# One ring of eight weight buffers, four split buffers and an even spread of the context's steps in a two-block network's expert stages

## The chip, the cores and the metric

The kernel runs on one NeuronCore of a Trainium2 chip. Its time is the device time of one execution in microseconds (us); lower is better. TensorE (PE) multiplies matrices, VectorE (DVE), ScalarE (ACT) and GpSimd (POOL) work on elements, and SyncE (SP) issues the DMA transfers that bring the weights from HBM into SBUF. Each engine takes its instructions strictly in the order in which they stand in its own queue.

## The reference, cut to what matters

Two blocks follow each other. The first runs on 256 tokens `x` of 1024 features: an RWKV layer and an attention layer, and behind each a mixture of experts. The second block begins with a feed-forward half-step on both `x` and a context `c` of 256 tokens; the context does not depend on the first block.

```python
def hier_moe(h, router_g, router_g_b, router_e, router_e_b, w_gate, w_up, w_down):
    # top-1 group of four, in it the top-2 of eight experts
    gates = ...                                   # (tokens, 4, 8), two of 32 not zero
    for gi in range(N_EXPERT_GROUPS):
        hid = jax.nn.silu(jnp.einsum('td,edf->tef', xt, w_gate[gi])) * jnp.einsum('td,edf->tef', xt, w_up[gi])
        hid = hid * gates[:, gi, :, None].astype(hid.dtype)
        out = out + jnp.einsum('tef,efd->td', hid, w_down[gi]).astype(f32)

def _ffn_half(h, g, shift, scale, gate, w_in, w_out):
    a, b = jnp.split(_modnorm(h, g, shift, scale) @ w_in, 2, axis=-1)
    return h + 0.5 * gate * ((jax.nn.silu(a) * b) @ w_out)
```

## The kernel before, in words

All weights lie in HBM as slots of 1 MiB (128 partitions of 2048 fp32). `K.slot` takes a buffer for the next slot and issues its DMA on SP's queue; `issue_after(self.last...)` chains the issues, so that the transfers are issued strictly in the order of the calls. An issue whose buffer is still being read waits, and all issues behind it wait too.

**An expert stage** (`moe`, called twice: after the RWKV layer, `moe0`, and after the attention layer, `moe1`) holds 96 expert slots: 32 experts in eight quads `q` = 0 to 7, 12 slots each. For a quad, `gate_up` multiplies eight slots into `ph` (line 1338, four matmuls of 512 columns a slot, fp32 weights read raw from the buffer). `experts` then computes `msg` = silu(gate) times up on ACT and DVE (lines 1399 and 1400), transposes it on PE into `cb` (line 1403; called T below), copies it to `hT` on ACT (line 1405), multiplies the four slots of the down projection into `py` (line 1411), and splits that into `yh` and `yl` on ACT and DVE (lines 1415 and 1416). After each odd quad 32 matmuls scatter the results of two quads back to the tokens (`cb`, lines 1425 and 1426), and DVE adds them to `X` (line 1427).

**The context's feed-forward half-step is the filler.** `side_ffn` is a generator of 33 steps in each expert stage, eleven times two input steps (`in_f_in`) and an output step (`in_f_out`). Each step takes one weight slot of its own and 48 matmuls of 256 columns. The product runs as three matmuls on pairs of a high and a low part (lines 135 to 137): a slot is split in four pieces of 512 columns, of each a high part `w` by a CAST on ACT (line 140) and a low part by a subtraction on DVE (line 141). The pieces live in the pool `spl`, two buffers. Two pairs of PSUM banks take the products (`fps`, `mps`). An input step ends with a silu on ACT (`sq`, line 343), a product on DVE (line 345) and the split of the result into `hh` (ACT) and `hl` (DVE), which the output step reads. `fill(n)` takes the next n steps; it is called after each second slot of `gate_up` and after the down projection, by the table `FILL` (a row for each quad, the fifth number after the down projection), and by `FRONT` in the first loads. The steps are emitted inside `tc.high_priority(offset=-30)`, which moves where the scheduler puts their instructions in the engines' queues relative to the experts'.

The expert slots rotate through the six buffers of the pool `mraw`, the context's slots through the three buffers of `K.raw`. When the first stage ends, `after()` computes the normalized input `u` of the context's next part (square sums, then for each of eight columns a product, `gs`, and the split `uh`, `ul`; lines 254 to 264). `load_ahead` issues the first slots of the following layer, and a branch (lines 1218 to 1220) skips the overflow loop.

Of the kernel before, what the change touches and what calls it, by code (L numbers as in the profile page):

```python
# [6 lines left out]
F32 = mybir.dt.float32  # L7
# [6 lines left out]
P = 128  # L14
# [12 lines left out]
class Pool:  # L27


    def __init__(self, pool, bufs, small):  # L30
        self.pool, self.bufs, self.small, self.sizes = pool, bufs, small, {}
# [23 lines left out]
@contextmanager  # L55
def sbuf(tc, name, bufs, small=False, side=None, **how):
    with tc.tile_pool(name=name, bufs=bufs, **how, **({"side": side} if side else {})) as p:
        q = Pool(p, bufs, small)
        yield q
        if not side:  # L60
            q.small = True
            q.align()


class Kern:


    def __init__(self, tc, ins, ctx):
        self.tc, self.nc, self.ins = tc, tc.nc, ins
        nc = self.nc  # L70
        ent = ctx.enter_context
        self.const = ent(sbuf(tc, reuse_waits="tile", name="const", small=True, bufs=1))
        self.raw = ent(sbuf(tc, reuse_waits="tile", name="raw", bufs=3))
        self.sm = ent(sbuf(tc, reuse_waits="tile", name="sm", small=True, bufs=2))
        self.nw = ent(sbuf(tc, reuse_waits="tile", name="nw", bufs=2))
        self.mp = ent(tc.tile_pool(reuse_waits="tile", name="mp", bufs=1, space=PSUM))
        self.const.pool.tile([P, 32], F32, name="first")
        self.ident = self.const.tile([P, P], F32, name="ident")
        nc.sync.dma_start(self.ident, ins["ident"])
        self.ones = self.const.tile([P, P], F32, name="ones")  # L80
        nc.vector.memset(self.ones, 1.0)
        self.last = self.spl = None
        self.ahead = {}

    def vec(self, name, n=8):
# [4 lines left out]
    def slot(self, stream, i, pool=None, to=None):  # L90
        if (stream, i) in self.ahead:
            return self.ahead.pop((stream, i))
        t = (pool or self.raw).tile([P, 2048], F32, name="raw") if to is None else to
        src = self.ins[stream][i]
        t = t[:, :src.shape[1]]
        if self.last and self.last[0] is self.nc.cur_bb:
            with self.tc.issue_after(self.last[1].ins):
                d = self.nc.sync.dma_start(t, src)
        else:
            d = self.nc.sync.dma_start(t, src)  # L100
        self.last = (self.nc.cur_bb, d)
        return t
# [1025 lines left out]
SOON = 60  # L1128

FRONT = (0, 0, 0, 0, 1, 1)  # L1130
FILL = [(0, 0, 0, 0, 1)] + [(1, 1, 1, 1, 1)] * 6 + [(0, 0, 0, 0, 0)]


def moe(K, mx, x, before, mods, gate, layer, s_w, side, after, ahead):

    nc, tc = K.nc, K.tc
    mm = nc.tensor.matmul
    with ExitStack() as ctx:
        mraw = ctx.enter_context(sbuf(tc, reuse_waits="tile", name="mraw", bufs=6 if side else 9))
        if side:  # L1140
            ctx.enter_context(K.splitting(2))
            ctx.enter_context(K.beside())
        ap = ctx.enter_context(sbuf(tc, reuse_waits="tile", name="mo1", small=True, bufs=1))
        loaded = {}

        def fill(n, late=30):
            with tc.high_priority(offset=-late):
                for _ in range(n if side else 0):
                    next(side, None)

        pos = ap.tile([P, 2, 32], F32, name="pos")
        gts = ap.tile([P, 2, 32], F32, name="gts")
        flag = ap.tile([P, 1], F32, name="flag")
        rt = ap.tile([P, 2], F32, name="rt")
        rw = ap.tile([P, 8, 36], F32, name="rw")
        nc.sync.dma_start(rw, K.ins["router"][layer])
        mc = ap.tile([P, 2 * P + 2 * 32 + 36 + 4], F32, name="mc")
        nc.sync.dma_start(mc, K.ins["moe_const"][layer])
        tri, iota, desc = mc[:, :P], mc[:, P:P + 32], mc[:, P + 32:P + 40]
        bias, sel4 = mc[:, P + 40:P + 76], mc[:, P + 76:P + 80]  # L1160

        def slot(i, to=None):
            if i in loaded:
                return loaded.pop(i)
            return K.slot(s_w, i, to=to, pool=None if 8 <= i % 12 < 11 and i < 84 and not side else mraw)


        gs, sh = mods
        rs = K.nw.tile([P, 8, 36], F32, name="sq")
        bt = ap.tile([P, 36], F32, name="bt")  # L1170
        nc.vector.tensor_mul(rs, rw, sh[:, :, None].to_broadcast([P, 8, 36]))
        nc.vector.tensor_mul(rw, rw, gs[:, :, None].to_broadcast([P, 8, 36]))
        ps = K.mp.tile([P, 36], F32, name="mps")
        for k in range(8):
            mm(ps, K.ones, rs[:, k], start=(k == 0), stop=(k == 7))
        nc.vector.tensor_add(bt, ps, bias)
        early = ExitStack()
        with tc.tile_pool(reuse_waits="tile", name="mop", bufs=1, space=PSUM) as pp, sbuf(tc, reuse_waits="tile", name="mo2", small=True, bufs=1) as wp:
            ps = pp.tile([P, 2, 36], F32, name="lp")
            ss = pp.tile([P, 2, 2], F32, name="ss")  # L1180
            before()
            xs = mx.tile([P, 8, 256], F32, name="m0")
            nc.gpsimd.tensor_copy(xs, x)
            lg = wp.tile([P, 2, 36], F32, name="lg")
            with tc.high_priority(offset=SOON):
                for k in range(8):
                    for t in range(2):
                        mm(ps[:, t], x[:, k, t * P:(t + 1) * P], rw[:, k], start=(k + t == 0), stop=(k == 7 and t == 1))
                K.square_sums(ss, x, 256)
                r = K.rsqrt_small(K.sm, ss[:, 0], 1.0 / 1024, EPS, 2, "rs")  # L1190
                nc.vector.tensor_copy(rt, r)
            for t in range(2):
                nc.vector.scalar_tensor_tensor(lg[:, t], ps[:, t], r[:, t:t + 1], bt, op0=OP.mult, op1=OP.add)
            gp = early.enter_context(sbuf(tc, reuse_waits="tile", name="mrt", bufs=1, side="right"))
            tokens = rows(K, gp, pp, x, rt)
            route(K, wp, lg, desc, pos, gts, pp, tri, flag)

        def between(b):
            for i in range(6 if side else 0):
                loaded[i] = slot(i)  # L1200
                fill(FRONT[i])
            for i in range(2):
                loaded[6 + i] = slot(6 + i, b[:, i])


        over = ap.tile([P, 8], F32, name="over")
        more = ap.tile([P, 1], I32, name="more")
        nc.vector.tensor_scalar(over, iota[:, :8], float(CAP), flag, op0=OP.mult, op1=OP.is_lt)
        nc.vector.tensor_reduce(flag, over[:, 1:], AX.X, OP.add)
        nc.vector.tensor_copy(more, flag)  # L1210
        dt = mx if layer else ap
        moe_round(K, dt, x, mods, gate, slot, pos, gts, iota, sel4, fill, between, (early, gp, tokens))
        fill(99)
        if after:
            after()
        K.load_ahead(ahead)
        with tc.issue_after(K.last[1].ins):
            n = nc.values_load(more[0:1, 0:1], min_val=0, max_val=7)
        with tc.If(n > 0):
            with tc.For_i(0, n):  # L1220
                nc.vector.tensor_scalar(pos, pos, -float(CAP), None, op0=OP.add)
                early = ExitStack()
                gp = early.enter_context(sbuf(tc, reuse_waits="tile", name="mrt", bufs=1, side="right"))
                with tc.tile_pool(reuse_waits="tile", name="mop", bufs=2, space=PSUM) as pp:
                    tokens = rows(K, gp, pp, xs, rt)
                moe_round(K, dt, x, mods, gate, slot, pos, gts, iota, sel4, lambda n: None, lambda b: None, (early, gp, tokens))
# [104 lines left out]
def gate_up(K, hp, slot, XT, q, fill):  # L1331

    ph = hp.tile([P, 512], F32, name="ph")
    for k in range(8):
# [5 lines left out]
        if k % 2:  # L1340
            fill(FILL[q][k // 2])
    return ph, m
# [48 lines left out]
def experts(K, wp, hp, x, gate, slot, phs, DT, XT, gsl, fill):  # L1391
    nc, tc = K.nc, K.tc
    mm = nc.tensor.matmul
    with tc.tile_pool(reuse_waits="tile", name="moe", bufs=1, space=PSUM) as pp, sbuf(tc, reuse_waits="tile", name="mor", bufs=2) as yp:
        ys = []
        for q in range(8):
# [20 lines left out]
            ys.append((yh, yl))  # L1417
            fill(FILL[q][4])
            if q % 2 == 1:
# [548 lines left out]
```

## Time and profile before

| | us |
|---|---|
| median of 3 runs | 3287.95 (3287.29 to 3293.46) |
| the profiled execution's own time | 3287.88 |
| its span in the profile | 3286.1 |
| first expert stage, first gate/up matmul to the last scatter | 752.2 to 1160.6 |
| second expert stage, the same | 1538.8 to 1949.6 |
| PE busy over the span | 3058.3 (93%) |
| DVE, ACT busy over the span | 1915.4 (58%), 1216.1 (37%) |
| mean of the DMA over the span | 199 GB/s |
| mean granted TensorE clock | 0.952 |

A view by windows gives, for a stretch of the span, the busy time of each engine with the number of its instructions, the granted clock, the mean busy share of the 16 DMA engines, and GB/s. A view of waits says which instruction waited for which, with the sum in us, the number of times and the longest. A row of the timeline is an instruction's start, its duration, engine, line, operation, output and inputs, and in brackets how long its engine had been idle before it and what ended that. The trace counts each matmul on raw fp32 weights twice, so a slot's four stand there as x8.

### The profile page before, as it was taken

The numbers are of one execution on the slowest core, as the hardware profiler recorded it, in microseconds if no ns is written. First come the engines' busy times: TensorE is split into PE (matmuls) and PEld (weight loads), VectorE is DVE, ScalarE is ACT, GpSimd is POOL, SyncE is SP. The second block draws the span as 40 slices with busy tenths as digits, with TensorE's granted clock in tenths as the row PEclk, the third lists the DMA queues.
The fourth block names the chain that finished last, engine by engine and source line by source line (L and its number), as shares of the span: only waits on it lengthen the run. The fifth ranks groups of instructions, "written<-read, shape, count | busy, mean of one in ns | idle before, by whom it ended". The sixth has DMA issues, their size and how long they took to land. (4 is left out here: it accounts for less than half of the span.)

```text
span 3286.1 us, 56989 instructions
## 1 busy us (share of the span) xinstructions
PE 3058.3 (93%) x23517; PEld 2490.1 (76%) x23517; DVE 1915.4 (58%) x4127; ACT 1216.1 (37%) x2560; POOL 212.7 (6%) x276
## 2 busy tenths in 40 slices
PE   5989999979998889999989979999999999999998
PEld 3765555566665579997666659999998888999998
DVE  4646665664444455555444448888865456544777
ACT  2532232233222245443322234455432223444443
POOL 1322232210000000000000000000000000000000
PEclk7889898989999989998999989999999999999999
DMA  7556676646888733345688764444532222232443
GB/s 262 190 193 220 228 267 212 244 178 263 339 324 328 303 126 142 129 146 233 273 339 322 309 254 185 172 165 170 190 116 90 103 90 91 103 105 101 167 181 115
DMA packets 98623, 654.59 MB, mean 199 GB/s; under 512 B 10672, under 2 KB 19760, under 8 KB 20400
## 3 DMA queue, kind: packets, MB, share of 16 engines
q1 hardware_dynamic: 95920, 648.73, 52.6%
q8 instruction: 188, 3.08, 0.4%
q10 hardware_dynamic: 2432, 2.10, 0.2%
q14 instruction: 83, 0.68, 0.1%
HBM read 649.74 MB, written 1.05 MB: 198 GB/s over the span
## 5 line engine op out<-in xcount | busy, mean ns | idle before, releaser
L140 ACT CAST w<-raw 128x512 fp32r<-128x512 f32 x1184 | 671.8, 618 | 760.9 <-issue 305.1
L141 DVE TENSOR_TENSOR w<-raw,w 128x512 fp32r<-128x512 f32 x1184 | 774.8, 688 | 291.8 <-ACT w L140 287.2
L135 PE MATMUL ab<-uh,w 128*128 128x258 f32 (+2 forms) x1440 | 446.3, 310 | 8.4 <-ACT uh L216 4.5
L136 PE MATMUL ab<-ul,w 128*128 128x258 f32 (+2 forms) x1440 | 446.3, 310 | 1.2 <-DVE ul L217 0.8
L137 PE MATMUL ab<-uh,w 128*128 128x258 f32 (+2 forms) x1440 | 445.9, 310 | 0.4 <-DVE w L141 0.4
L135 PEld LDWEIGHTS ab<-uh,w 128*128 128x128 f32 x1440 | 277.2, 193 | 23.0 <-ACT uh L216 5.5
L136 PEld LDWEIGHTS ab<-ul,w 128*128 128x128 f32 x1440 | 277.5, 193 | 14.7 <-DVE ul L217 1.4
L137 PEld LDWEIGHTS ab<-uh,w 128*128 128x128 f32 x1440 | 277.5, 193 | 13.3 <-DVE w L141 0.9
L135 PE MATMUL po<-hh,w 128*128 128x256 f32 (+1 forms) x736 | 223.8, 304 | 0.5 <-DVE X L383 0.4
L136 PE MATMUL po<-hl,w 128*128 128x256 f32 (+1 forms) x736 | 221.0, 300 | 0.0
L137 PE MATMUL po<-hh,w 128*128 128x256 f32 (+1 forms) x736 | 221.1, 300 | 0.0
L462 PE MATMUL mps<-raw,cst 128*32 128x512 f32 x960 | 191.1, 694 | 25.8 <-DMA raw<-in_ada 20.5
L383 DVE SCALAR_TENSOR_TENSOR X<-po,ga,X 128x256 f32<-128x256 f32 x440 | 196.5, 479 | 18.3 <-PE po L137 17.3
L135 PEld LDWEIGHTS po<-hh,w 128*128 128x128 f32 x736 | 138.7, 188 | 7.2 <-DVE X L383 1.0
L136 PEld LDWEIGHTS po<-hl,w 128*128 128x128 f32 x736 | 139.0, 189 | 5.9 <-DVE hl L141 0.2
L137 PEld LDWEIGHTS po<-hh,w 128*128 128x128 f32 x736 | 138.5, 188 | 5.6
L135 PE MATMUL mps<-uh,w 128*128 128x256 f32 x384 | 112.5, 293 | 13.4 <-ACT w L140 13.4
L137 PE MATMUL fps<-uh,w 128*128 128x256 f32 x384 | 112.9, 294 | 11.9 <-DVE w L141 11.5
L136 PE MATMUL rp<-ul,w 128*128 128x256 f32 (+1 forms) x400 | 119.1, 298 | 2.0 <-POOL ul L264 1.8
L135 PE MATMUL rp<-uh,w 128*128 128x256 f32 (+1 forms) x400 | 118.4, 298 | 1.3 <-ACT uh L263 1.3
L137 PE MATMUL rp<-uh,w 128*128 128x256 f32 (+1 forms) x400 | 118.4, 296 | 0.0
L135 PE MATMUL fps<-uh,w 128*128 128x256 f32 x384 | 112.8, 294 | 4.7 <-ACT w L140 4.7
(606 smaller groups left out, 6907.4 us busy)
## 6 DMA issues: line engine op xcount, KB each, us to landing
raw<-in_moe SPq DMA_DIRECT2D x188, 1024.0 KB, 7.6
raw<-in_f_in SPq DMA_DIRECT2D x132, 1024.0 KB, 4.8
raw<-in_w_mod SPq DMA_DIRECT2D x72, 1024.0 KB, 5.1
raw<-in_f_out SPq DMA_DIRECT2D x66, 1024.0 KB, 4.9
raw<-in_ada SPq DMA_DIRECT2D x48, 1024.0 KB, 5.9
raw<-in_qkv SPq DMA_DIRECT2D x36, 1024.0 KB, 4.8
raw<-in_ret_in SPq DMA_DIRECT2D x24, 1024.0 KB, 4.8
raw<-in_fnet SPq DMA_DIRECT2D x8, 1024.0 KB, 4.8
```

Of the source, the lines that this page charges most:

```text
L135: mm(out, lh, rh, start=start, stop=False)
L136: mm(out, lh, rl, start=False, stop=False)
L137: mm(out, ll, rh, start=False, stop=stop)
L140: self.nc.scalar.copy(hi, src)
L141: self.nc.vector.tensor_sub(lo, src, f32(hi))
L383: nc.vector.scalar_tensor_tensor(x[:, m, c], po[:, p], g[:, m:m + 1], x[:, m, c], op0=OP.mult, op1=OP.add)
L462: nc.tensor.matmul(ps[32 * j:32 * j + 32], K.cst[:, which, k], raw[:, j * 512:(j + 1) * 512], start=(k == 0), stop=(k == 7))
```

## The change

The loads of experts and context take their buffers from one ring of eight, in the order of use, where there were six for the experts and three for the context. The split pieces get four buffers in place of two. The context's steps lose their priority offset, and the table `FILL` spreads the same 33 steps evenly, four a quad and none after the down projection.

```diff
         self.last = self.spl = None
+        self.ring = []
...
-        t = (pool or self.raw).tile([P, 2048], F32, name="raw") if to is None else to
+        if to is None:
+            if self.ring and not pool:
+                pool = self.ring[0]
+                self.ring.append(self.ring.pop(0))
+            to = (pool or self.raw).tile([P, 2048], F32, name="raw")
+        t = to
...
-FILL = [(0, 0, 0, 0, 1)] + [(1, 1, 1, 1, 1)] * 6 + [(0, 0, 0, 0, 0)]
+FILL = [(0, 1, 0, 1, 1)] + [(1, 1, 1, 1, 0)] * 7
...
-        mraw = ctx.enter_context(sbuf(tc, reuse_waits="tile", name="mraw", bufs=6 if side else 9))
-        if side:
-            ctx.enter_context(K.splitting(2))
-            ctx.enter_context(K.beside())
+        mraw = ctx.enter_context(sbuf(tc, reuse_waits="tile", name="mraw", bufs=5))
+        ctx.enter_context(K.splitting(4))
+        ctx.enter_context(K.beside())
+
+        K.ring = [K.raw, mraw, mraw, K.raw, mraw, mraw, K.raw, mraw]
...
-        def fill(n, late=30):
-            with tc.high_priority(offset=-late):
-                for _ in range(n if side else 0):
-                    next(side, None)
+        def fill(n):
+            for _ in range(n):
+                next(side, None)
...
-            return K.slot(s_w, i, to=to, pool=None if 8 <= i % 12 < 11 and i < 84 and not side else mraw)
+            return K.slot(s_w, i, to=to, pool=None if K.ring else mraw)
...
+        K.ring.clear()
         K.load_ahead(ahead)
```

Three places show what this does to the engines' orders; line numbers behind the change are six or seven higher. The first is PE's order in quad 3 of the first stage: `ph` are the experts' gate/up matmuls (four a slot), `py` the down projection of quad 2, `fps` and `mps` the context's. Before, around the third and the fourth slot:

```order
2645 L136 MATMUL mps<-ul,w 128x256
2646 L137 MATMUL mps<-uh,w 128x256
2647 L1338 MATMUL ph<-raw,XTa 32x512 x4
2648 L135 MATMUL mps<-uh,w 128x256
2649 L136 MATMUL mps<-ul,w 128x256
...
2665 L137 MATMUL mps<-uh,w 128x256
2666 L135 MATMUL mps<-uh,w 128x256
2667 L1338 MATMUL ph<-raw,XTa 32x512 x4
2668 L136 MATMUL mps<-ul,w 128x256
2669 L137 MATMUL mps<-uh,w 128x256
```

And now, around the first four slots:

```order
2611 L143 MATMUL fps<-uh,w 128x256
2612 L1418 MATMUL py<-raw,hT 32x512 x16
2613 L1345 MATMUL ph<-raw,XTa 32x512 x8
2614 L141 MATMUL mps<-uh,w 128x256
2615 L142 MATMUL mps<-ul,w 128x256
...
2660 L142 MATMUL mps<-ul,w 128x256
2661 L143 MATMUL mps<-uh,w 128x256
2662 L1345 MATMUL ph<-raw,XTa 32x512 x8
2663 L141 MATMUL fps<-hh,w 128x256
2664 L142 MATMUL fps<-hl,w 128x256
```

Before, every gate/up slot stands alone, with 19 or 29 context matmuls on either side, in the middle of a step. Now two slots run together, mostly at the border between two steps, and a whole step of 48 lies between two such runs (one pair in four stands as 1 and 7 matmuls, on either side of half an output step).

The second place is ACT's order in quads 2 and 3 of the first stage: `sq` is the silu that ends an input step, `w` the splits of the context's slots, and `msg`, `hT` and `yh` belong to the experts. Before:

```order
543 L140 CAST w<-raw 128x512 x4
544 L343 ACTIVATE sq<-fps 128x256
545 L140 CAST w<-raw 128x512 x2
546 L140 CAST hh<-sq 128x256
547 L140 CAST w<-raw 128x512 x2
548 L343 ACTIVATE sq<-mps 128x256
549 L140 CAST w<-raw 128x512 x2
550 L140 CAST hh<-sq 128x256
551 L140 CAST w<-raw 128x512 x6
552 L1399 ACTIVATE msg<-ph 128x256
```

And now:

```order
546 L146 CAST w<-raw 128x512 x8
547 L349 ACTIVATE sq<-fps 128x256
548 L146 CAST hh<-sq 128x256
549 L1406 ACTIVATE msg<-ph 128x256
550 L146 CAST w<-raw 128x512 x4
551 L1412 COPY hT<-cb 128x256
552 L349 ACTIVATE sq<-mps 128x256
553 L146 CAST hh<-sq 128x256
554 L1422 ACTIVATE yh<-py,gsl 128x1024
555 L146 CAST w<-raw 128x512 x8
```

The first two splits of a step stood between the silu of the step before it and its `hh`; now all four of a step stand behind `hh`, and for some steps eight stand together.

The third place is the end of the first expert stage on ACT: `uh` are the eight columns of the context's next normalization, `d` the splits of the constants that the following layer begins with, and `more` the load of the branch's flag. Before:

```order
611 L172 ACTIVATE sq<-X 128x512 x3
612 L263 CAST uh<-sq 128x256 x8
613 L1399 ACTIVATE msg<-ph 128x256
614 L1405 COPY hT<-cb 128x256
615 L1415 ACTIVATE yh<-py,gsl 128x1024
616 L1218 TENSOR_LOAD more
```

And now:

```order
599 L178 ACTIVATE acc<-X 128x512
600 L178 ACTIVATE sq<-X 128x512 x3
601 L1422 ACTIVATE yh<-py,gsl 128x1024
602 L269 CAST uh<-sq 128x256 x2
603 L1225 TENSOR_LOAD more
...
639 L146 CAST d<-raw 128x256 x2
640 L269 CAST uh<-sq 128x256
641 L146 CAST d<-raw 128x256 x3
642 L269 CAST uh<-sq 128x256
643 L146 CAST hh<-fps 128x512
644 L178 ACTIVATE acc<-X 128x512
```

All eight columns stood ahead of the last quad's `msg`; now none does, two stand behind the last `yh`, and six behind the branch, among the first instructions of the attention layer.

## Rows read from the trace of the kernel before

**Rows 1.** Windows: first stage by quads 0–1, 2–3, 4–5, 6–7; then quads 2–3 of the second.

```profile
core 0: us, PE busy (x) PEld busy (x) DVE busy (x) ACT busy (x) POOL busy (x), PEclk, DMA share, GB/s
752.20:840.60 88.40, 83.23 (x586) 59.51 (x584) 35.14 (x66) 26.71 (x52) 0.00 (x0) 0.92 0.81 336
840.60:952.60 112.00, 99.75 (x711) 68.06 (x709) 48.71 (x91) 31.85 (x60) 0.00 (x0) 0.98 0.84 329
952.60:1062.10 109.50, 98.21 (x708) 67.79 (x707) 50.98 (x97) 31.21 (x58) 0.00 (x0) 0.98 0.84 327
1062.10:1160.60 98.50, 79.55 (x528) 48.72 (x526) 44.60 (x95) 25.46 (x48) 3.62 (x5) 0.91 0.68 260
...
1628.00:1740.00 112.00, 99.80 (x710) 68.63 (x708) 48.88 (x90) 31.74 (x60) 0.00 (x0) 0.98 0.90 351
```

**Rows 2.** Windows: a stretch of the first stage's opening, and one within quad 2.

```profile
760.00:800.00 40.00, 40.00 (x296) 29.67 (x289) 18.72 (x34) 14.36 (x26) 0.00 (x0) 1.00 1.01 424
880.00:890.00 10.00, 8.89 (x67) 6.31 (x66) 5.63 (x13) 3.23 (x7) 0.00 (x0) 1.00 0.96 348
```

**Rows 3.** Waits of PE in the first stage: total us, times, longest.

```profile
PE cb L1403 <- DVE msg L1400: 9.1, 2, 7.8
PE fps L135 <- ACT w L140: 8.6, 8, 1.7
PE mps L135 <- ACT w L140: 6.2, 6, 1.7
PE fps L137 <- DVE w L141: 5.5, 7, 1.3
PE cb L1425 <- ACT yh L1415: 4.9, 4, 1.2
PE cb L1426 <- DVE yl L1416: 3.6, 5, 0.8
PE mps L137 <- DVE w L141: 2.0, 6, 0.9
```

**Rows 4.** Waits of SP's queue in the first stage.

```profile
SPq L98 <- DVE w L141: 111.7, 11, 17.8
```

**Rows 5.** Timeline of PE in quads 2 and 3 of the first stage.

```profile
890.68 1.92 PE L1411 MATMUL py<-raw,hT 128*32 128x512 f32 x16
...
903.99 0.28 PE L137 MATMUL fps<-uh,w 128*128 128x256 f32 x1
...
905.03 0.28 PE L137 MATMUL fps<-uh,w 128*128 128x256 f32 x1
...
906.28 0.39 PE L135 MATMUL mps<-uh,w 128*128 128x256 f32 x1 [0.98 <-ACT w L140]
...
907.01 0.39 PE L137 MATMUL mps<-uh,w 128*128 128x256 f32 x1 [0.22 <-DVE w L141]
...
909.03 1.06 PE L1338 MATMUL ph<-raw,XTa 128*32 128x512 f32 x8
...
915.89 0.39 PE L135 MATMUL fps<-hh,w 128*128 128x256 f32 x1 [0.98 <-ACT w L140]
```

**Rows 6.** Timeline of ACT at the wait of 906.28.

```profile
905.34 0.38 ACT L343 ACTIVATE sq<-fps 128x256 f32<-128x256 f32 x1 [3.37 <-PE fps L137]
905.62 1.13 ACT L140 CAST w<-raw 128x512 fp32r<-128x512 f32 x2
906.65 0.41 ACT L140 CAST hh<-sq 128x256 fp32r<-128x256 f32 x1
```

**Rows 7.** Timeline of DVE there, and at the first stage's end.

```profile
905.75 0.42 DVE L345 TENSOR_TENSOR sq<-sq,fps 128x256 f32<-128x256 f32 x1 [3.06 <-ACT sq L343]
...
1132.73 0.42 DVE L254 TENSOR_TENSOR sq<-X,mps 128x256 f32<-128x256 f32 x1 [1.38 <-PE mps L188]
...
1144.04 0.41 DVE L261 TENSOR_SCALAR sq<-sq,gs,mod 128x256 f32<-128x256 f32 x1
```

**Rows 8.** Timeline of ACT behind the first stage's branch, and of PE at the attention layer's first projection.

```profile
1164.12 1.63 ACT L140 CAST d<-raw 128x256 fp32r<-128x256 f32 x5 [10.73 <-PEq L1219]
...
1182.05 0.51 PE L135 MATMUL pj<-uh,w 128*128 128x256 f32 x2 [0.98 <-ACT uh L263]
```

More of the change, by code (lines that the diff above doesn't have):

```diff
@@ L1198, in between @@
         def between(b):
-            for i in range(6 if side else 0):
+            for i in range(6):
                 loaded[i] = slot(i)
```

## The prediction, made before the changed kernel ran

> **What bounds the kernel now.** I read the windows first. PE is busy 93% of the span, so only its idle time and its slow stretches can be won back, and the change touches only the two expert stages, 408.4 and 410.8 us long. In the first, quads 2–3 and 4–5 take 112.0 and 109.5 us with about 12 us of idle PE each; quads 6–7, with half as many context steps, still take 98.5 us, 19 of them idle, at a granted clock of 0.91 [rows 1]. The second stage has the same pair, 112.0 us with 99.80 busy.
>
> Next the waits of PE. Four rows name the split pieces `w`, 22.3 us in all and over 14 steps; the results `yh` and `yl` cost 8.5 us; one wait for `msg` cost 7.8 us [rows 3]. No row of that list names a weight slot that has not landed. Yet the transfers are not far off: over 40 us in the opening they moved 424 GB/s at a share of 1.01 [rows 2], a 1 MiB slot every 2.47 us, and over a pair they are at a share of 0.84 [rows 1]. SP's queue in turn waited 111.7 us for the context's splits to free a buffer [rows 4].
>
> The timeline shows why the splits are late. At 906.28 and at 915.89 PE begins a piece after 0.98 us of idle time that ended with ACT's CAST; between them lie 48 context matmuls and two lone expert slots, 9.61 us [rows 5]. ACT began that CAST at 905.62, directly behind the silu of the step before, which itself had waited for PE's last matmul of that step [rows 6]. There are two split buffers, half a slot, so ACT cannot have all the next slot's pieces done while the running step still reads two of them; and what it does is queued behind that silu.
>
> **The step, costed.** Nine matmuls of a step start 1.04 us after one another in sum (903.99 to 905.03, [rows 5]), 0.1156 us each, so 48 take 5.55 us; with a change of operand 5.7. Two expert slots without a break take 1.92 us (`py`, 890.68), a lone one 1.06. Two slots and a step would thus be 7.6 us where 9.61 passed: 1.5 us of it the gaps at 906.28 and 907.01 (their 0.98 and 0.22 with the drain of the matmul before), 0.5 the breaks in and out of lone slots.
>
> With four buffers the four splits of a step stand behind the `hh` of an earlier one and can run while a whole step and two expert slots pass. A step's four CASTs take 2.3 us on ACT (twice 1.13), and ACT and DVE are busy 32 and 49 us of the 112 [rows 1], so both have room. Where no step lies between, the run of two expert slots is the cover: 1.92 us against silu 0.38, product 0.42, `hh` 0.41 and the first CAST, 0.6 [rows 6, 7], together 1.8. It is just enough, so I leave 0.2 us a step; if that cover went, the loss would be the 1.5 of today.
>
> **A pair of quads after the change** has eight steps, not ten: 8 × 5.7 and 8 × 0.2 make 47.2; eight runs of two gate/up slots 15.2, and 4 more because one in four is cut in 1 and 7 and the scatter cuts some further; eight down slots 8.2; 32 scatter matmuls 3.7 and a break each way, 4.7; transposes 0.8. New waits: T follows `ph` directly in the odd quads and with little between in the even, where 9 context matmuls covered it, so it waits for `msg` (the uncovered one in [rows 3] is 9.1 less 7.8, 1.3 us); I take 2.2 for two. `yl` and one split behind the scatter come to 1.9 (today's `yh` and `yl` are 8.5 over four scatters, 2.1). That is 84 us; the clock was at 0.98 in both pairs [rows 1], which is 2 us, and stays so: 86. The transfers of its 32 slots need 79 us at 2.47, close enough that I add 1 for their unevenness: **87 us**.
>
> **A stage.** The opening gets one step more: 88.4 + 6 = 94.4. Three pairs are 261, and the last quad's chain behind its last slot 3. That makes 358 us against 408, **50 less**. Half of that comes from the end: a fourth pair of 98.5 us for five steps becomes one of 87 for eight, because steps cover its experts, and because in the first stage `msg` no longer stands behind eight normalization columns, 1132.73 to 1144.04 [rows 7]. The second stage's pairs have the same length and no such columns, but its end had idle time too; I take 50 there as well.
>
> **What is given back.** Six of those eight columns now lie behind the branch, between the `d` splits with which the attention layer begins. They took 11.7 us for eight, 1.46 each [rows 7], at most 8.8 for six. Between the branch and the first projection lie 17.9 us (1164.12 to 1182.05, [rows 8]) in which ACT and DVE are not full. Below zero is excluded, since nothing leaves that stretch; I take 5. Sum: 3287.9 − 100 + 5 = 3193, rounded up to **3195 us**; the profiled execution and the median of the runs differ by 0.1 us.
>
> Terms without a row: the leftover at a step lies between 0 and 1.5 us (26 steps a stage: −5 to +34), and it is nearest to 0 since the covers above add up; the breaks of the cut runs between 1.5 and 7 us a pair. The issue orders of the loads ahead of either stage change by two or three slots; the `mraw` pool is filled while the router runs, so I cost them at nothing; a slot that came late would cost 2.5 us, one transfer. The forecast's own range is 3170 to 3225.
>
> **Rivals.**
>
> *The transfer becomes the bound.* In 880 to 890 the DMA was at a share of 0.96 and moved only 348 GB/s [rows 2], 3.0 us a slot. At that rate three pairs need 96 × 3.0 = 288 us, or 264 if eight slots are in hand when they begin: 3 to 27 us a stage above the 261, in all 3201 to 3249. Middle: 3228. Against it stand the 424 GB/s over 40 us, at full share, with the same transfers. Chance 0.15.
>
> The Trainium skill speaks against the change here: "DMA: Bandwidth & Descriptors", section Specifications, gives an HBM limit of about 358 GB/s for a core, an estimated 2.93 us a slot, with which this rival would hold throughout. The trace disagrees, since 424 GB/s lasted for 40 us [rows 2]; by that, the forecast holds.
>
> *The splits stay late.* ACT's order is only regrouped: where eight CASTs stand behind one `hh`, a `yh` or `hT` waits behind up to 2.3 us of them, and a split waits for its own slot as now. Then 17 us of split waits a stage and the breaks stay, and only the end of each stage gains, some 13 us: 3262. For it: DVE, which makes the low parts, is the busier of the two, 49 us of a pair against 32 [rows 1], and its rows end the later gaps [rows 3]. Chance 0.12.
>
> *All waits vanish*, also T's and the scatter's, and the clock never falls: a pair of 80 us, the time of its transfers: 3195 − 6 × 7 = 3153. Chance 0.07.
>
> *Slower: the one ring stops behind the context.* Eight buffers in order of use replace nine in two pools. A context slot is freed only by its fourth subtraction, and SP already lost 111.7 us to that [rows 4], while experts had their own six. If the ring stands still behind each context slot, what arrives sets the time: a stage has 129 slots, ten of them there at its start, and 408 us over 119 slots are 3.43 us each. Above that spacing the change loses; at 3.6, a context slot held for the 0.7 us more that four late pieces would cost over four slots, the stage takes 428 and the kernel 3330. Against it: four split buffers let the pieces go earlier than now. Chance 0.05.
>
> *No effect worth the name*, the gains at the steps given back at T, the scatter and the branch: 3288. Chance 0.03.
>
> **How the numbers follow.** The forecast has 0.58. Its range, the transfer rival and the best case hold 0.80; 3160 to 3250 takes them in. A measurement of this kernel tells 0.2%, 6.6 us, from no change. Faster are the forecast, the transfer, the late splits and the best case, 0.92, less 0.02 for the late splits' upper end: 0.90; the same 0.04; slower 0.06.
>
> **What would show it.** Right: split waits of a few us a stage in place of 22; pairs near 87 us and all three alike; no wait of 7.8 us at the first stage's end; DMA share in the pairs above 0.9; new waits of about 1 us at T; the stretch from the branch to the first projection longer by some 5 us. Wrong: PE waiting for `raw` slots in the pairs at a share near 1 (the transfer); waits for `w` still near 20 us (late splits); SP's waits for `w` grown, with a share below 0.8 (the ring stands still).

## The result and the profile after

The changed kernel took 3171.27 us (median of 4, 3167.14 to 3176.66) against 3288.4: a ratio of 0.9644 (0.9629 to 0.9658), 117 us faster. Forecast were 3195 us and a range of 3160 to 3250. The profiled execution is the slowest of the four, 3176.66 us with a span of 3174.9, 111.2 us below the span of before.

The windows of the changed kernel cut both expert stages at the first gate/up matmul of quads 0, 2, 4 and 6, and at the last scatter (columns as in [rows 1]):

```profile
745.90:836.80 90.90, 89.25 (x662) 66.18 (x660) 40.44 (x78) 30.01 (x61) 0.00 (x0) 0.94 0.74 299
836.80:923.60 86.80, 80.67 (x616) 56.30 (x614) 39.16 (x73) 26.55 (x53) 0.00 (x0) 1.00 0.98 401
923.60:1010.40 86.80, 81.28 (x613) 56.10 (x612) 41.33 (x79) 24.45 (x50) 0.00 (x0) 1.00 0.96 390
1010.40:1107.10 96.70, 88.69 (x650) 62.53 (x648) 51.61 (x108) 27.67 (x54) 0.73 (x1) 0.96 0.80 322
1492.60:1574.80 82.20, 82.18 (x650) 61.18 (x648) 38.53 (x74) 29.67 (x59) 0.00 (x0) 1.00 0.76 311
1574.80:1658.80 84.00, 79.21 (x617) 55.79 (x615) 38.98 (x73) 26.68 (x53) 0.00 (x0) 1.00 1.01 426
1658.80:1745.40 86.60, 81.08 (x613) 55.98 (x612) 41.27 (x79) 24.39 (x49) 0.00 (x0) 1.00 0.96 397
1745.40:1838.20 92.80, 86.39 (x640) 60.48 (x638) 45.50 (x86) 24.38 (x48) 0.00 (x0) 0.98 0.85 340
```

A middle pair of quads (2–3, 4–5) takes 84 to 87 us where 112.0 and 109.5 stood [rows 1], at a DMA share near 1. The first stage is 361 us long, not 408; the second 346, not 411. From the first stage's last scatter to the attention layer's first projection 28 us pass, not 21.5. Another 6 us came ahead of the first stage (its first matmul starts at 745.9, not 752.2), on work that the change leaves alone. One kernel's executions spread that far: in the profile of the changed kernel's second set of runs (`after_again` below) that matmul starts at 737.8.

PE's waits in the first stage of the changed kernel, the answer to [rows 3]:

```profile
PE cb L1410 <- DVE msg L1407: 6.9, 7, 1.2
PE fps L143 <- DVE w L147: 3.0, 4, 0.9
PE mps L143 <- DVE w L147: 2.7, 6, 0.9
PE cb L1432 <- ACT yh L1422: 2.5, 2, 1.2
PE cb L1433 <- DVE yl L1423: 1.9, 1, 1.9
```

The split waits are 5.7 us, from 22.3, and none of them is on ACT. The wait of 7.8 us for `msg` is gone; seven of about 1 us have come. PE's timeline shows one period, from one run of two expert slots to the next:

```profile
852.32 1.92 PE L1345 MATMUL ph<-raw,XTa 128*32 128x512 f32 x16
...
855.00 0.38 PE L143 MATMUL mps<-uh,w 128*128 128x256 f32 x1 [0.22 <-DVE w L147]
...
860.62 1.92 PE L1345 MATMUL ph<-raw,XTa 128*32 128x512 f32 x16
```

It takes 8.30 us, where the same work took 9.61 [rows 5].

The chain behind the first stage, on PE:

```profile
1111.21 0.58 PE L141 MATMUL fps<-d,uh 128*128 128x256 f32 x1 [4.20 <-ACT d L146]
...
1116.01 0.58 PE L141 MATMUL fps<-d,uh 128*128 128x256 f32 x1 [2.90 <-DVE hl L147]
...
1119.92 0.55 PE L141 MATMUL mps<-d,hh 128*128 128x256 f32 x1 [2.26 <-ACT w L146]
...
1124.16 0.36 PE L141 MATMUL mps<-d,hh 128*128 128x256 f32 x1 [1.33 <-DVE ul L147]
...
1135.09 0.50 PE L141 MATMUL pj<-uh,w 128*128 128x256 f32 x2 [0.98 <-ACT uh L269]
```

### The profile page after: what moved, and what is told of

Its sections match the earlier page's. It is cut to its first block, busy times and chain, and to the rows that moved or that the text cites. A ratio compares the mean times of both kernels' runs of the same rounds, so it can differ in the third digit from the quotient of the medians.

```text
span 3174.9 us, 56904 instructions
## 1 busy us (share of the span) xinstructions
PE 2995.9 (94%) x23517; PEld 2477.1 (78%) x23517; DVE 1911.5 (60%) x4127; ACT 1206.6 (38%) x2560; POOL 212.8 (7%) x276
## 5 line engine op out<-in xcount | busy, mean ns | idle before, releaser
L146 ACT CAST w<-raw 128x512 fp32r<-128x512 f32 x1184 | 661.0, 618 | 507.3 <-issue 304.7
L147 DVE TENSOR_TENSOR w<-raw,w 128x512 fp32r<-128x512 f32 x1184 | 764.9, 689 | 139.4 <-ACT w L146 135.0
L143 PE MATMUL fps<-uh,w 128*128 128x256 f32 x384 | 108.8, 283 | 3.0 <-DVE w L147 2.8
L351 DVE TENSOR_TENSOR hf<-sg,ab 128x512 f32<-128x512 f32 x22 | 15.1, 688 | 160.0 <-ACT sg L349 160.0
```

The source lines that it names most:

```text
L143: mm(out, ll, rh, start=False, stop=stop)
L146: self.nc.scalar.copy(hi, src)
L147: self.nc.vector.tensor_sub(lo, src, f32(hi))
L351: nc.vector.tensor_mul(hf, sg, pb)
```

## The experiments

**Theory A** is the prediction's: a step lost time to splits that came late for want of buffers, and to breaks around lone slots. **Theory B**: the ring feeds PE, and the transfers are what bounds. **Theory C**: the order of the queues, moved by the dropped priority offset, is what pays, and buffers matter little. **Theory D**, for one run: the two pools cost because they change PE's order. Ratios are to the kernel before, run beside each on the same chip; where one is turned into us it is multiplied by 3288. An edit can move the scheduler's order of PE's queue too; where a reading hangs on that, the text says so.

**The changed kernel again**, as the base of the runs with r9s2.

> The changed kernel once more, to be compared on one chip with the next: every theory says 0.9644 of before, within 0.2%.

3169.74 us, ratio 0.965 (0.9634 to 0.9666).

**One part undone: the split buffers.**

```diff
-        ctx.enter_context(K.splitting(4))
+        ctx.enter_context(K.splitting(2))
```

> The changed kernel with two split buffers in place of four, all else as changed. Theory A (the step's own cost: splits that PE waits for, and breaks between lone slots): the 22 us of split waits a stage return, 3171 + 2 x 17 = about 3205, at least 3195. Theory B (the ring feeds PE: eight buffers in order of use keep the transfers going): the ring is still there, so within 10 us of 3171. Theory C (the order of PE's queue, from the dropped priority offset): within 10 us as well.

0.9705 (0.9684 to 0.9727), 20 us slower than the changed kernel, short of the 24 that A asked for and over the 10 of B and C. A's cause does not show in the trace: its profiled execution, the fastest of its four (3177 us, the others 3185 to 3190), had the same list of waits in the first stage, with 4.8 us for splits and none on ACT. So two buffers do not bring back the 22 us of split waits. PE's order is not quite the same, most of all in the openings of the two stages, and the second stage is 351 us long in the profile, 5 more than the changed kernel's; where the other executions lost their time no profile shows.

**One part undone: the ring.**

```diff
-        K.ring = [K.raw, mraw, mraw, K.raw, mraw, mraw, K.raw, mraw]
+        K.ring = []
```

> The changed kernel without the ring: five buffers for the experts and three for the context, in two pools, all else as changed. Theory A: within 10 us of 3171, since no row of before shows PE waiting for a slot that had not landed. Theory B: the DMA share in the pairs falls from 0.98 to about 0.85, the pairs go to 100 us or more, 3171 + 6 x 13 = 3250. Theory C: within 10 us.

0.9848 (0.9818 to 0.9877), 67 us slower: theory B's direction, though not its 100 us a pair, and against A. Its pairs in the first stage, and what PE waited for in them:

```profile
840.30:930.40 90.10, 81.52 (x613) 56.88 (x612) 38.86 (x73) 25.41 (x50) 0.00 (x0) 0.98 0.91 377
930.40:1022.30 91.90, 83.66 (x614) 58.15 (x613) 41.45 (x79) 24.72 (x48) 0.00 (x0) 0.96 0.89 366
```

```profile
PE ph L1345 <- DMA raw<-in_moe: 3.1, 2, 1.6
...
PE mps L141 <- ACT w L146: 2.1, 1, 2.1
PE fps L141 <- ACT w L146: 2.1, 1, 2.1
```

From quad 2 on PE's order is that of the changed kernel but for a few rows at the start of quad 2, so these 3 to 5 us a pair come from the pools: PE waits for expert slots that have not landed and for splits of slots that came late, 16 us of waits in the two pairs for 11, while the share falls to 0.9 and the granted clock to 0.98 and 0.96. The two stages together are 54 us longer than the changed kernel's. Some 23 of these lie in the openings (101.5 and 95.1 us for 90.9 and 82.2), where PE's order is another; the pairs and the ends, in the same order, make up 31.

**One part undone: the table.**

```diff
-FILL = [(0, 1, 0, 1, 1)] + [(1, 1, 1, 1, 0)] * 7
+FILL = [(0, 0, 0, 0, 1)] + [(1, 1, 1, 1, 1)] * 6 + [(0, 0, 0, 0, 0)]
```

> The changed kernel with the old table FILL (five steps a quad in the middle, one in the first, none in the last). Theory A: the end of each stage loses its cover, some 13 us a stage, about 3195. Theory B: a last pair with fewer context slots is simply shorter, and the middle pairs longer, within 10 us. Theory C: within 15 us.

0.9761 (0.9725 to 0.9796), 38 us slower; A, but more than it said. The last pair of the first stage:

```profile
1037.00:1123.20 86.20, 71.56 (x491) 44.30 (x490) 42.94 (x94) 22.85 (x45) 3.62 (x5) 0.88 0.77 291
```

It has 14.6 us of idle PE, and a clock of 0.88; the pair ahead of it, with ten steps, takes 102.5 us. The last pair has `msg` behind the normalization columns again, a wait of 6.9 us, and the stretch from the last scatter to the attention layer's first projection is 20.7 us: what the changed kernel pays there it saves here.

**One part undone: the offset.**

```diff
         def fill(n):
-            for _ in range(n):
-                next(side, None)
+            with tc.high_priority(offset=-30):
+                for _ in range(n):
+                    next(side, None)
```

> The changed kernel with the priority offset of -30 around the context's steps put back. Theory A: the breaks return, 0.5 us at each of 26 steps a stage, and no split waits: 3171 + 26 = about 3197. Theory B: within 10 us. Theory C: the order of before returns and with it most of the gain is lost, 3240 or more.

0.986 (0.9832 to 0.9888), 71 us slower: theory C. With ring, table and four buffers in place, its first stage has these waits:

```profile
PE fps L143 <- DVE w L147: 8.4, 9, 1.3
PE fps L141 <- ACT w L146: 5.8, 6, 1.0
PE mps L141 <- ACT w L146: 4.9, 5, 1.0
PE mps L143 <- DVE w L147: 4.3, 14, 0.9
```

23.4 us, as much as before the change, although there are four buffers. ACT's rows at one of these waits show why the four do not help:

```profile
842.61 0.38 ACT L349 ACTIVATE sq<-fps 128x256 f32<-128x256 f32 x1 [16.04 <-PE fps L143]
842.89 2.17 ACT L146 CAST w<-raw 128x512 fp32r<-128x512 f32 x4
```

For 16.04 us ACT stood idle until PE's last matmul of the step let the silu run; all four CASTs of the next step stand right behind that silu in its queue. PE, which has nothing between the two steps in this order, then waits 0.98 us for the first of them. The splits are late because of where they stand in the queues. The waits are 17.7 us above the changed kernel's in this stage; twice that is half of the 71, and the rest was not taken apart.

**The memory of two split buffers as a ninth ring buffer.**

```diff
-        mraw = ctx.enter_context(sbuf(tc, reuse_waits="tile", name="mraw", bufs=5))
-        ctx.enter_context(K.splitting(4))
+        mraw = ctx.enter_context(sbuf(tc, reuse_waits="tile", name="mraw", bufs=6))
+        ctx.enter_context(K.splitting(2))
...
-        K.ring = [K.raw, mraw, mraw, K.raw, mraw, mraw, K.raw, mraw]
+        K.ring = [K.raw, mraw, mraw] * 3
```

> The changed kernel with the memory of two split buffers given to the ring: nine buffers, two split buffers. If four split buffers carry the gain (theory A), 15 to 20 us slower than the changed kernel. If the ring's feed carries it (theory B), the ninth buffer makes up for them: within 6 us of it, or up to 10 faster.

3179.75 us, 0.9684 (0.966 to 0.9709), between the two forecasts: in the median 10 us behind the changed kernel on the same chip, with runs from 3170 to 3191. The changed kernel stays ahead; whether the ninth buffer made up for some of the 20 us of the two, these runs cannot tell.

**Half of each expert slot, with the ring and without.**

```diff
+        if stream[:3] == "moe":
+            src = src[:, :1024]
...
-   raw[:, j * 512:(j + 1) * 512]
+   raw[:, j % 2 * 512:(j % 2 + 1) * 512]
```

> The changed kernel, but of each expert slot only the first half is loaded (512 KiB), and the matmuls of the third and fourth expert of a quad read the weights of the first and second: the same matmuls, 20 slots' worth of transfer a pair in place of 32. If the pairs of 87 us are now bound by the transfers (theory B, share 0.96 to 1.01), they fall to what PE needs, about 80 us, and the time by 6 x 7 = 40 to about 3130. If they are bound by PE's own chain, within 10 us of the changed kernel.

> Two pools of five and three buffers in place of the ring, with the same halved loads. Theory B (two pools starve the transfers): the 67 us of the missing ring vanish, within 10 us of the halved kernel with the ring. Theory D (the two pools change PE's order, and that order costs): at least 40 us of them stay.

3121.39 us (0.95) and 3167.46 us (0.9638). The pairs of the first of the two kernels fell to 78.7 to 81.6 us at a share near 0.75, as B said. But in both kernels the scheduler put the transposes behind a step instead of ahead of it, so the seven waits for `msg` went too, and the two causes are not told apart here. That the missing ring still costs 46 us speaks for D: they lie in the openings (96 and 94 us against 81 and 78), where PE's order differs, and at the ends, not in the pairs between. With whole slots, though, 31 of the 54 us stood in stretches of one and the same order, so D is not the whole of it.

**More bytes in an unchanged order.**

```diff
+        waste = ap.tile([P, 512], F32, name="waste")
...
         def fill(n):
             for _ in range(n):
+                nc.gpsimd.dma_start(waste, K.ins[s_w][0][:, :512])
                 next(side, None)
```

> The changed kernel with one more load of 256 KiB in front of each of the context's steps, on GpSimd's queue into a tile that nobody reads: PE's order stays row for row, a pair of quads moves the bytes of 34 slots in place of 32. If the transfers set the pairs' 87 us (theory B), two slots more cost 5 us a pair and 66 loads of 0.6 us in all about 40 us: 3210. If PE's own chain sets them (theory A), at most 10 us: 3180.

3585.83 us (1.0905), but that number says nothing: the last `fill(99)` of a stage calls 99 times, so a stage issued 132 such loads, one behind the other, and the layer behind waited for the rest (197.2 us in one wait). Within the first stage they ran beside the weights all the time, and in both stages PE's order is unchanged. Its windows in the first stage, and one of the second with what PE waited for in it:

```profile
836.50:922.70 86.20, 80.06 (x616) 55.71 (x616) 39.22 (x73) 25.95 (x51) 6.98 (x13) 1.00 1.01 425
922.70:1009.20 86.50, 81.02 (x611) 55.95 (x610) 40.86 (x78) 24.60 (x48) 6.44 (x12) 1.00 1.01 425
...
1791.60:1881.10 89.50, 81.03 (x615) 57.48 (x614) 39.02 (x73) 26.17 (x51) 6.71 (x13) 0.98 1.01 425
```

```profile
PE mps L141 <- ACT w L146: 2.8, 1, 2.8
...
PE ph L1348 <- DMA raw<-in_moe: 1.6, 1, 1.6
```

In the first stage a pair carried three slots' worth more (13 and 12 loads of 256 KiB) at 425 GB/s, and took 86.2 and 86.5 us as without them, with the same waits of PE. So PE's chain sets those pairs, with the transfers at their heel. In the second stage, where quads 2–3 took 84.0 us at a share of 1.01, the same load cost 5.5 us, 4.4 of them the two waits shown, for an expert slot that had not landed and for a split; neither stands in the changed kernel's list there. With the loads the transfers set that pair's pace. Quads 4–5 of the second stage took 86.6 us again, as without the loads.

**One part done alone, on the kernel before: no offset; four split buffers (and five for the experts); the ring** (each the edit above, from the other side).

> The kernel before with one edit: no priority offset around the context's steps. Theory C (the order of the queues is what the change moves): most of the split waits go without more buffers, 50 to 80 us faster, 3210 to 3235. Theory A (they need the four buffers): the breaks alone, about 20 us, 3265.

> The kernel before with four split buffers, and five buffers for the experts in place of six to pay for them. Theory A: 17 us of split waits a stage go, 3250. Theory C: the splits still stand behind the silu in ACT's queue, within 10 us of 3285, and the missing sixth buffer may cost some.

> The kernel before with the ring of eight buffers in place of six and three, two split buffers, the old table and the old offset. Theory B (the feed): 40 us faster or more. Theory C: the ring pays only when PE's order lets it be quick, within 10 us of 3285.

No offset: 0.9805 (0.9763 to 0.9847), 64 us faster. Four split buffers: 1.0099 (1.0066 to 1.0131), 33 us slower. The ring: 1.0004 (0.9979 to 1.0029), no change. The first and the last are theory C's. Four split buffers go against theory A, but 33 us is more than the 10 that C left them: the edit takes a buffer from the experts too and moves PE's order in the openings, and the runs do not part these. The first stage of the kernel with no offset and two split buffers has 7.0 us of split waits, in three rows:

```profile
PE fps L135 <- ACT w L140: 3.5, 2, 1.7
...
PE mps L137 <- DVE w L141: 1.8, 5, 0.9
...
PE mps L135 <- ACT w L140: 1.7, 1, 1.7
```

Its first pair after the opening takes 99.7 us, with ten steps of the context as before. With four buffers and the old order the split waits stay:

```profile
PE fps L135 <- ACT w L140: 9.2, 9, 1.7
...
PE mps L135 <- ACT w L140: 6.0, 6, 1.7
...
PE fps L137 <- DVE w L141: 4.3, 6, 1.0
...
PE mps L137 <- DVE w L141: 3.4, 13, 0.9
```

## Why the prediction was right, and where not

**The time lay in the range, for partly another reason.** The waits named (splits, the lone slots' breaks, `msg` behind the columns) are those that went, and a pair came to 86.8 us where 87 was worked out. The step that failed is "There are two split buffers, half a slot, so ACT cannot have all the next slot's pieces done", and the paragraph that lets four buffers cure it. The runs put the order in its place: without the offset two buffers leave 7.0 us of split waits, with it four leave 22.9 and 23.4. Alone the dropped offset gives 64 of the 117 us.

The other half of that sentence, that the CAST is queued behind the silu, is right, and it holds without the offset too. PE and ACT in the kernel with no offset and two split buffers:

```profile
891.50 1.92 PE L1337 MATMUL ph<-raw,XTa 128*32 128x512 f32 x16
...
894.18 0.39 PE L137 MATMUL mps<-uh,w 128*128 128x256 f32 x1 [0.22 <-DVE w L141]
```

```profile
891.60 0.38 ACT L343 ACTIVATE sq<-fps 128x256 f32<-128x256 f32 x1 [2.32 <-PE fps L137]
892.47 0.41 ACT L140 CAST hh<-sq 128x256 fp32r<-128x256 f32 x1 [0.49 <-DVE sq L345]
892.78 1.14 ACT L140 CAST w<-raw 128x512 fp32r<-128x512 f32 x2
```

The CASTs wait for the silu and `hh` as before. What is new is that PE has two expert slots to multiply between the steps, 1.92 us, where before it went from one step straight to the next; the wait of 0.98 us for ACT is gone, and 0.22 for DVE is left. The changed kernel has the same order: beside the two slots at 852.32, shown above, ACT's silu starts at 852.43, `hh` at 853.30 and the four CASTs at 853.61. This cover the prediction had costed (1.92 us against 1.8), so that part of the mechanism came true; the four buffers it set beside the cover were not what cured the waits. What they give in the changed kernel, 20 us, shows in no list of waits, and its cause stays open.

**The ring has no gain of its own in the sum and is worth 67 us in the end.** Alone it changes nothing: PE with its breaks and late splits still took 112.1 and 109.5 us for a pair in that run, for which the pools were quick enough. When a pair takes 87, they are not: that is the 31 us in pairs and ends. The openings' 23 us go with another order of PE, and the runs do not say what of them is order and what is feed. The parts' prices do not add up: undone singly, they come to 20 + 67 + 38 + 71 = 196 us.

**The terms.** The step with its two slots was worked out as 7.6 us, 7.8 with the leftover, and took 8.30, with 0.22 for a split still in it. The pair of quads came out all the same, and that is luck. Adding up the distances from each PE start to the next in quads 2–3, the context's matmuls took 48.5 us for 45.6 (8 × 5.7), and the rest came close: expert slots 26.7 for 27.4, scatter 5.4 for 4.7, waits 5.7 for 5.7. What paid for the 3 us was the margin, 2 us for a clock of 0.98 (granted was 1.00) and 1 for uneven transfers.

The first stage was to lose 50 us and lost 47. "Half of that comes from the end" does not follow from the prediction's own sum, where the end gives 98.5 − 90 = 8.5 us; it gave 1.8. The last pair took 97, not 90, and so not all pairs are alike: 58 scatter matmuls stand in it, 11.3 us, where quads 4–5 have 32 and 5.2, and the term for the chain behind the last slot (3 us) has no room for them.

The second stage was to lose 50 and lost 65. The mis-sized term is its opening, taken as long as the first's. In the kernel before it was longer; its quads 0–1, 2–3 and 6–7:

```profile
1538.80:1639.20 100.40, 96.66 (x605) 59.66 (x603) 37.17 (x69) 27.45 (x54) 0.00 (x0) 0.98 0.71 282
1639.20:1751.20 112.00, 99.74 (x711) 68.96 (x709) 48.95 (x91) 31.84 (x60) 0.00 (x0) 0.98 0.89 347
...
1860.70:1949.50 88.80, 75.64 (x518) 47.02 (x516) 32.42 (x60) 19.79 (x36) 0.00 (x0) 0.94 0.74 293
```

The last window of [rows 1], called quads 2–3, begins at 1628.0 and so 11 us too early: by it the opening would be 89 us. The length of the pair is the same. Behind the change the opening is 82.2 us with more context matmuls in it (650 PE instructions for 605), while the last pair is 4 us longer than before, not shorter. The opening's timeline in the kernel before shows what was there:

```profile
1540.50 4.50 PE L1338 MATMUL ph<-raw,XTa 128*32 128x512 f32 x40
1544.93 0.38 PE L137 MATMUL mps<-uh,w 128*128 128x256 f32 x1
1545.24 1.04 PE L1338 MATMUL ph<-raw,XTa 128*32 128x512 f32 x2
1546.22 0.39 PE L135 MATMUL mps<-uh,w 128*128 128x256 f32 x1
1546.54 1.04 PE L1338 MATMUL ph<-raw,XTa 128*32 128x512 f32 x2
```

Twenty expert matmuls in one run took 4.43 us, 0.22 each; then single ones alternate with single context matmuls, at 1.30 us for the two. From 1545.24 to 1566.05 sixteen single ones stand like this; in the changed kernel's opening only one stands alone. Against 0.22 and the context matmul's 0.116 in a run, sixteen at 1.30 are an estimated 15 us, most of the 18.2 by which the two openings differ.

Two numbers of the prediction are off without weight: the middle of 3201 and 3249 is 3225, not 3228, and the best case, 3153, lies outside the range that was to take it in.

**What was given back** behind the branch was put at 5 us and is 6.6 (28.1 less 21.5). New in PE's waits are those for `hl`, `w` and `ul` of the attention layer's own splits (2.90, 2.26 and 1.33 us), between which the columns now stand on ACT and DVE, as costed; `d` and `uh` were waited for before as well (4.08 and 0.98), and one wait of 3.19 us for that layer's square sums is gone.

**The rivals.** The transfers were near: share 0.96 to 1.01, but at 390 to 426 GB/s and not at 348, and PE waited for no slot in the pairs; only with more bytes did they set one, quads 2–3 of the second stage. The Trainium skill's limit of about 358 GB/s ("DMA: Bandwidth & Descriptors", section Specifications) does not hold here: in the run with more bytes 425 GB/s lasted a whole pair, 86.2 us. The late splits fell with 5.7 us of waits. The ring that stops behind the context did not come: SP's waits for `w` went from 111.7 [rows 4] to 81.7 us in 29 short ones, none over 8.9.

## What to carry to other kernels

A wait that looks like a shortage of buffers may be a place in a queue: see what stands ahead of the awaited instruction on its engine, and what the waiting engine has to do in the meantime. Change the order first, then count buffers. Undo each part of a change as well as doing it alone, since a part that gives nothing by itself (the ring) can come to half of the gain once another has made the consumer faster. Keep the pieces of a filler whole, and size each stage's opening and end from its own rows, cut at the instruction that begins it, not from another stage's.

## What the runs showed of the hardware

A lone matmul of a raw fp32 slot's quarter costs nearly as much as the slot's four: one took 1.04 us (at 1545.24), four 1.06 as a run [rows 5], eight 1.92, and twenty 4.50. The four write to separate quarters of `ph`'s partitions; the timing fits with their running side by side, which no run here tests by itself. Cutting such a group therefore costs far more here than the change of operand that I had reckoned with (0.15 us a step).
